# Two output products: making the last operands of a seven-product matmul inside its first group

## The chip, the cores and the metric

The kernel runs on one core of a Trainium2 chip. Its time is the device time of one execution in microseconds (us); three runs gave a median of 2010.18 us (2009.14 to 2012.45). The engines that matter here are TensorE (PE in the profile; its weight loads are PEld), VectorE (DVE), ScalarE (ACT), GpSimd (POOL) and SyncE (SP), which here only issues loads.

## The reference, cut to what matters

The reference is a small encoder trunk on an input x of 512 tokens by 2048 channels, all in float32. One layer (A) is a gated linear recurrence, one layer (B) is an attention with a forget gate; B takes its keys and values from the stream after A. Each layer ends in the same way, and only this end is touched:

```
o = head_rmsnorm(o, out_norm_w)              # 512 x 2048
o = o.reshape(B, T, D_MODEL) * silu(gate)
return x + (o @ w_out)                       # w_out: 2048 x 2048
```

There are two such output products, one per layer.

## The kernel before, in words

All activations lie transposed: 16 tiles of 128 channels by 512 tokens. For the matmuls each operand is split, in the type float32r, into a high part (ScalarE casts it: `xh`, `wh`) and a low part (VectorE subtracts the high part: `xl`, `wl`), and each product is made of three matmuls: high by high, low by high, high by low. Both steps of the split stand in the helper `split`, so all casts have line L444 and all subtractions L445, whatever they split.

An output product has two stages.

**The plain group.** `group` makes output rows 0 to 511 in the ordinary way: 16 contraction tiles, four banks `gm0` to `gm3`, three matmuls of 512 columns each, 192 matmuls (L242 to L244). Its callback `before(kt)` splits the activation tile `y{kt}` into `xh{kt}` and `xl{kt}`, and after each odd kt it calls `quick_prep` for the pair (kt-1, kt).

**Six seven-product groups.** The other 1536 output rows are made 256 at a time by a scheme that does a 2 by 2 block product with seven block products instead of eight. The contraction is cut into 8 pairs p of tiles. For each pair the scheme needs, beside quarters of the two activation tiles, three sums of quarters (`th{p}`, `tl{p}`) and a fourth that overwrites the second half of `xh`, `xl` of the even tile. `quick_prep` makes them: four subtractions of 128x256 on VectorE into a buffer `wm` (L261 to L264), then the split of three of them (128x768: `th`, `tl`) and of the fourth (128x256: into `xh`, `xl`). The weights come in chunks of 512 KB, each for two pairs: three coefficient blocks are used as loaded, four are sums. Per chunk, VectorE makes the sums (`w_sums`: L156 on 128x512, L157 and L158 on 128x256, into another `wm` buffer), and both kinds are split separately: the loaded ones as 128x768, the sums as 128x1024, all into the two tiles `w7h`, `w7l`. One pair is 21 matmuls of 256 columns (L296 to L298), one group 168, a product's six groups 1008. At the end of each group `quick_sum` combines the seven results on VectorE.

**Buffers.** Weights as loaded (`wr`) have two buffers, `w7h` and `w7l` two each, `wm` two, which operands and weight sums share. A chunk's load can start only when the chunk two before has been read; a split into `w7h` can start only when PE has finished with the chunk two before.

**What sets the order.** The program is written as one stream; a scheduler puts it into an order on each engine before the kernel is built, by its own estimate of when things are ready. Within an engine the order is then fixed: an instruction that waits holds all that stand behind it on that engine. In `quick`, the load of a chunk, its split, and then the matmuls are written pair by pair; the callback `make` of the change is called between the split and the matmuls.

## Time and profile before

| | |
|---|---|
| median of 3 runs | 2010.18 us |
| the profiled execution | 2011.1 us |
| its span | 2009.4 us |
| mean granted PE clock over the span | 0.995 |
| PE busy | 98% of the span |
| VectorE busy | 78% |
| ScalarE busy | 56% |
| PE share of the chain that ended last | 83% |

The span runs from the first to the last recorded instruction; 1.7 us of the execution lie outside it. A timeline row reads: start in us, duration in us, engine, line, operation, output <- input, shape, count, and in square brackets the engine's idle time before it with what ended it. On PE and VectorE the next instruction starts somewhat before the one ahead has ended, so what counts in a sequence is the distance from start to start. The seven-product groups of the first output product lie at 893 to 1028 us, those of the second at 1869 to 2002 us.

### The profile page before, as it was taken

The numbers are of one execution on the slowest core, as the hardware profiler recorded it, in microseconds if no ns is written. First come the engines' busy times: TensorE is split into PE (matmuls) and PEld (weight loads), VectorE is DVE, ScalarE is ACT, GpSimd is POOL, SyncE is SP. The second block draws the span as 40 slices with busy tenths as digits, with TensorE's granted clock in tenths as the row PEclk, the third lists the DMA queues.
The fourth block names the chain that finished last, engine by engine and source line by source line (L and its number), as shares of the span: only waits on it lengthen the run. The fifth ranks groups of instructions, "written<-read, shape, count | busy, mean of one in ns | idle before, by whom it ended". The sixth has DMA issues, their size and how long they took to land.

```text
span 2009.4 us, 28900 instructions
## 1 busy us (share of the span) xinstructions
PE 1978.4 (98%) x10218; PEld 1695.3 (84%) x10218; DVE 1558.7 (78%) x3321; ACT 1130.1 (56%) x2311; POOL 207.3 (10%) x365
## 2 busy tenths in 40 slices
PE   9999999999999999989999999999999999999898
PEld 7888888888888888879987888888888888888898
DVE  7969987979798889797893677776766676687877
ACT  6646655657566466653464555665555556576332
POOL 3303110203122030010000000000000000000100
PEclk9999999999999999999999999999999999999999
DMA  5222222222222222243432222322223332323443
GB/s 190 74 88 81 74 84 74 84 78 80 83 76 74 74 84 84 84 155 120 157 118 95 95 87 87 95 90 94 85 89 90 94 95 90 90 84 106 137 157 105
DMA packets 57600, 195.01 MB, mean 97 GB/s; under 512 B 7904, under 2 KB 8032, under 8 KB 57456
## 3 DMA queue, kind: packets, MB, share of 16 engines
q1 hardware_dynamic: 52192, 176.39, 28.0%
q0 software_dynamic: 5120, 16.78, 2.5%
q8 instruction: 80, 1.31, 0.3%
q14 instruction: 64, 0.52, 0.1%
q10 hardware_dynamic: 144, 0.01, 0.0%
HBM read 184.73 MB, written 8.42 MB: 96 GB/s over the span
## 4 chain that ended last, share of the span: by engine, by line
PE 83%; DVE 7%; DMA 5%; issue 3%; ACT 1%; POOL 1%; SPq 0%; POOLq 0%; DVEq 0%; ACTq 0%
PE gm L244 17%; PE gm L242 17%; PE gm L243 17%; PE gm L238 6%; PE gm L240 6%; PE gm L239 6%; DMA wr<-in_wa_q 3%; DVE w7l L445 2%; PE mx L594 2%; PE mx L593 2%; PE mx L592 1%; DMA wr<-in_wb_q 1%; PE mx L439 1%; PE mx L440 1%; PE mx L438 1%
## 5 line engine op out<-in xcount | busy, mean ns | idle before, releaser
L242 PE MATMUL gm<-xh,wh 128*128 128x512 f32 x1664 | 650.5, 392 | 0.1
L243 PE MATMUL gm<-xl,wh 128*128 128x512 f32 x1664 | 650.2, 391 | 0.0
L244 PE MATMUL gm<-xh,wl 128*128 128x512 f32 x1664 | 610.8, 392 | 0.2 <-DVE wl L445 0.2
L243 PEld LDWEIGHTS gm<-xl,wh 128*128 128x128 f32 x1664 | 313.2, 188 | 62.8
L242 PEld LDWEIGHTS gm<-xh,wh 128*128 128x128 f32 x1664 | 313.3, 188 | 62.6 <-DVE z L390 0.3
L244 PEld LDWEIGHTS gm<-xh,wl 128*128 128x128 f32 x1664 | 312.0, 188 | 62.6 <-DVE wl L445 0.9
L444 ACT CAST wh<-wr 128x512 fp32r<-128x512 f32 x288 | 177.3, 621 | 155.2 <-PE gm L243 112.7
L445 DVE TENSOR_TENSOR wl<-wr,wh 128x512 fp32r<-128x512 f32 x288 | 204.8, 714 | 67.2 <-ACT wh L444 57.3
L147 ACT ACTIVATE wh<-wr,v_b_norm_w 128x256 fp32r<-128x256 f32 (+1 forms) x192 | 111.6, 584 | 187.1 <-PE gm L243 152.1
L148 DVE SCALAR_TENSOR_TENSOR wl<-wr,v_b_norm_w,wh 128x256 fp32r<-128x256 f32 (+1 forms) x192 | 109.3, 570 | 131.6 <-ACT wh L147 126.4
L239 PE MATMUL gm<-wl,xh 128*128 128x512 f32 x512 | 200.2, 392 | 0.0
L240 PE MATMUL gm<-wh,xl 128*128 128x512 f32 x512 | 199.3, 392 | 0.0
L238 PE MATMUL gm<-wh,xh 128*128 128x512 f32 x512 | 179.6, 393 | 2.4 <-DVE q L556 1.6
L147 ACT ACTIVATE wh<-wr,v_kv_norm_w 128x256 fp32r<-128x256 f32 (+1 forms) x192 | 110.0, 573 | 56.1 <-PE gm L240 44.1
L148 DVE SCALAR_TENSOR_TENSOR wl<-wr,v_kv_norm_w,wh 128x256 fp32r<-128x256 f32 (+1 forms) x192 | 109.2, 570 | 32.7 <-ACT wh L147 32.1
L587 DVE COPY_PREDICATED at<-masks,mx 128x128 f32<-128x128 uint8 (+4 forms) x448 | 108.4, 296 | 13.6 <-PE mx L594 13.2
L238 PEld LDWEIGHTS gm<-wh,xh 128*128 128x128 f32 x512 | 95.8, 188 | 22.1 <-DVE q L556 1.9
L240 PEld LDWEIGHTS gm<-wh,xl 128*128 128x128 f32 x512 | 96.2, 188 | 19.0
L239 PEld LDWEIGHTS gm<-wl,xh 128*128 128x128 f32 x512 | 96.3, 188 | 18.8
L953 POOL TENSOR_SCALAR_AFFINE_SELECT s<-s 128x128 f32<-128x128 f32 x64 | 28.4, 444 | 741.6 <-DVE s L952 741.1
L444 ACT CAST w7h<-wr 128x768 fp32r<-128x768 f32 x48 | 40.1, 835 | 114.5 <-PE mx L297 48.8
L444 ACT CAST kh<-k 128x512 fp32r<-128x512 f32 (+1 forms) x96 | 56.4, 587 | 44.2 <-PE mx L593 19.0
(232 smaller groups left out, 3879.8 us busy)
## 6 DMA issues: line engine op xcount, KB each, us to landing
wr<-in_wb_qk SPq DMA_DIRECT2D x64, 512.0 KB, 3.5
wr<-in_wa_qf SPq DMA_DIRECT2D x62, 512.0 KB, 3.5
wr<-in_wa_v SPq DMA_DIRECT2D x32, 512.0 KB, 3.5
wr<-in_wa_g SPq DMA_DIRECT2D x32, 512.0 KB, 3.5
wr<-in_wb_v SPq DMA_DIRECT2D x32, 512.0 KB, 3.6
wr<-in_wb_g SPq DMA_DIRECT2D x32, 512.0 KB, 3.5
wr<-in_wa_q SPq DMA_DIRECT2D x24, 512.0 KB, 3.5
wr<-in_wb_q SPq DMA_DIRECT2D x24, 512.0 KB, 3.6
```

What stands on the lines that cost most here:

```text
L147: S.activation(h[:, c], r[:, c], AF.Copy, scale=w[:, kt : kt + 1])
L148: V.scalar_tensor_tensor(l[:, c], r[:, c], w[:, kt : kt + 1], rd(h)[:, c], op0=ALU.mult, op1=ALU.subtract)
L238: PE.matmul(banks[j], xh, h, start=f, stop=False)
L239: PE.matmul(banks[j], xh, l, start=False, stop=False)
L240: PE.matmul(banks[j], xl, h, start=False, stop=e)
L242: PE.matmul(banks[j], h[:, c], Xh[kt], start=f, stop=False)
L243: PE.matmul(banks[j], h[:, c], Xl[kt], start=False, stop=False)
L244: PE.matmul(banks[j], l[:, c], Xh[kt], start=False, stop=e)
L444: S.copy(h, src)
L445: return V.tensor_sub(l, src, rd(h))
L587: V.copy_predicated(out, mv, data)
L593: PE.matmul(lv[:, base : base + n], kh[:, c], ml, start=False, stop=False)
```

## The change

In the plain group the callback now makes the operands of pairs 0 to 4 only (after kt 1, 3, 5, 7 and 9). Those of pairs 5, 6 and 7 are made in the first seven-product group, one in each of its first three pair steps, between the weight split and the matmuls of that step. No arithmetic is added or removed, and each operand is still made by the same instructions.

```
     def quick(banks, prep, evac, hold, make=None):
...
             if not (wts.parts or hold and p == KT // 2 - 1):
                 wts.split()
+            if make:
+                make()
             th, tl, _ = prep[p]
...
-            end = quick(banks, prep, lambda *p, k=k, r=r: evac(k, r, p), hold and u == 5)
+            end = quick(banks, prep, lambda *p, k=k, r=r: evac(k, r, p), hold and u == 5, None if u else make)
...
+        def make():
+
+            if len(prep) < KT // 2:
+                prep.append(quick_prep(len(prep), Yd))
+                prep[-1][2]()
+
         def before(kt):
             y_split(kt)
-            if kt % 2:
-                prep.append(quick_prep(kt // 2, Yd))
-                prep[-1][2]()
+            if kt % 2 and kt < 10:
+                make()
```

The scheduler turns this into another order around the border between the two stages of each output product, and nowhere else. In the rows below, buffers have their numbers. The first weight chunk of the first output product is `wr_1873`, `w7h_1896`, `w7l_1897` before and `wr_1870`, `w7h_1887`, `w7l_1888` after; the second is `w7h_1904` before and `w7h_1898` after; the third, fourth and fifth are `w7h_1908`, `w7h_1912` and `w7h_1916` in both. Lines from the first edit on are two higher after the change (the split is L446 and L447).

VectorE at the border of the first output product, before: the last two of the four additions that empty the plain group's banks, the last two operands, and then the sums of the first two weight chunks together.

```order
L824 TENSOR_TENSOR y2_1920_9950<-gm2_1797_9288,z_1790_9275 128x512
L824 TENSOR_TENSOR y3_1921_9953<-gm3_1798_9289,z_1791_9277 128x512
L445 TENSOR_TENSOR tl6_1882_9644<-wm_1880_9638,th6_1881_9643 128x768
L445 TENSOR_TENSOR tl7_1894_9697<-wm_1892_9691,th7_1893_9696 128x768
L156 TENSOR_TENSOR wm_1895_9702<-wr_1873_9612 128x2x256
L156 TENSOR_TENSOR wm_1903_9751<-wr_1885_9665 128x2x256
L157 TENSOR_TENSOR wm_1895_9702<-wm_1895_9702,wr_1873_9612 128x2x128
L157 TENSOR_TENSOR wm_1903_9751<-wm_1903_9751,wr_1885_9665 128x2x128
L158 TENSOR_TENSOR wm_1895_9702<-wm_1895_9702,wr_1873_9612 128x2x128
L158 TENSOR_TENSOR wm_1903_9751<-wm_1903_9751,wr_1885_9665 128x2x128
L445 TENSOR_TENSOR w7l_1897_9707<-wm_1895_9702,w7h_1896_9706 128x2x512
L445 TENSOR_TENSOR w7l_1905_9756<-wm_1903_9751,w7h_1904_9755 128x2x512
```

The same engine after the change, from the last subtraction of pair 4 on: the first chunk's sums and both of its splits stand here, ahead of the low parts of pair 5, and the four additions come after four more rows.

```order
L264 TENSOR_TENSOR wm_1856_9532<-y9_1114_5706,wm_1856_9532 128x256
L156 TENSOR_TENSOR wm_1886_9669<-wr_1870_9601 128x2x256
L447 TENSOR_TENSOR w7l_1888_9674<-wr_1870_9601,w7h_1887_9673 128x2x384
L157 TENSOR_TENSOR wm_1886_9669<-wm_1886_9669,wr_1870_9601 128x2x128
L447 TENSOR_TENSOR wl_1883_9650<-wr_1861_9559,wh_1882_9649 128x512
L447 TENSOR_TENSOR tl4_1858_9538<-wm_1856_9532,th4_1857_9537 128x768
L158 TENSOR_TENSOR wm_1886_9669<-wm_1886_9669,wr_1870_9601 128x2x128
L261 TENSOR_TENSOR wm_1894_9697<-y10_1236_6344 128x256
L262 TENSOR_TENSOR wm_1894_9697<-y10_1236_6344,y11_1331_6803 128x256
L263 TENSOR_TENSOR wm_1894_9697<-y11_1331_6803,wm_1894_9697 128x256
L264 TENSOR_TENSOR wm_1894_9697<-y11_1331_6803,wm_1894_9697 128x256
L447 TENSOR_TENSOR w7l_1888_9674<-wm_1886_9669,w7h_1887_9673 128x2x512
```

ScalarE at the same border, before and after. `w7h<-wr` casts a chunk's loaded coefficients, `w7h<-wm` its sums.

```order
L444 CAST xh14_1886_9667<-wm_1892_9691 128x256
L444 CAST th6_1881_9643<-wm_1880_9638 128x768
L444 CAST th7_1893_9696<-wm_1892_9691 128x768
L444 CAST w7h_1896_9706<-wm_1895_9702 128x2x512
L444 CAST w7h_1904_9755<-wm_1903_9751 128x2x512
L444 CAST w7h_1908_9809<-wr_1902_9728 128x2x384
L444 CAST w7h_1908_9809<-wm_1907_9805 128x2x512
L444 CAST w7h_1912_9863<-wr_1906_9782 128x2x384
```

```order
L446 CAST w7h_1908_9809<-wr_1893_9695 128x2x384
L446 CAST w7h_1898_9733<-wm_1897_9729 128x2x512
L446 CAST th6_1901_9744<-wm_1900_9739 128x768
L446 CAST xh14_1880_9645<-wm_1904_9773 128x256
L446 CAST w7h_1912_9863<-wr_1903_9771 128x2x384
L446 CAST th7_1905_9778<-wm_1904_9773 128x768
L446 CAST w7h_1908_9809<-wm_1907_9805 128x2x512
L446 CAST w7h_1912_9863<-wm_1911_9859 128x2x512
L446 CAST w7h_1916_9917<-wr_1910_9836 128x2x384
```

In the order after, the cast of the third chunk's loaded coefficients stands ahead of the cast of the second chunk's sums, and the fourth's ahead of the third's; before, no cast of a later chunk's loaded coefficients stood ahead of an earlier chunk's sums in these rows.

VectorE after the change, some 20 rows behind the four additions:

```order
L447 TENSOR_TENSOR w7l_1913_9864<-wr_1903_9771,w7h_1912_9863 128x2x384
L447 TENSOR_TENSOR tl7_1906_9779<-wm_1904_9773,th7_1905_9778 128x768
L447 TENSOR_TENSOR w7l_1909_9810<-wm_1907_9805,w7h_1908_9809 128x2x512
L156 TENSOR_TENSOR wm_1911_9859<-wr_1903_9771 128x2x256
L156 TENSOR_TENSOR wm_1915_9913<-wr_1910_9836 128x2x256
L157 TENSOR_TENSOR wm_1911_9859<-wm_1911_9859,wr_1903_9771 128x2x128
L157 TENSOR_TENSOR wm_1915_9913<-wm_1915_9913,wr_1910_9836 128x2x128
L158 TENSOR_TENSOR wm_1911_9859<-wm_1911_9859,wr_1903_9771 128x2x128
L158 TENSOR_TENSOR wm_1915_9913<-wm_1915_9913,wr_1910_9836 128x2x128
L447 TENSOR_TENSOR w7l_1913_9864<-wm_1911_9859,w7h_1912_9863 128x2x512
```

Here too the fourth chunk's coefficients and the last operand stand ahead of the low part of the third chunk's sums, and the first sum of the fifth chunk stands ahead of the last two of the fourth. The second output product has the same order with other buffer numbers.

More of the change, by code (lines that the diff above doesn't have):

```diff
@@ L268, in quick_prep, with quick @@
         return th, tl, lambda: split(m[:, 0, :], Xh[k1][:, TN:], Xl[k1][:, TN:])
-    def quick(banks, prep, evac, hold):
+    def quick(banks, prep, evac, hold, make=None):
         half = lambda i: banks[i // 2][:, (i % 2) * TN : (i % 2 + 1) * TN]
@@ L315, in quick_sum, with quick_groups @@
         V.tensor_add(o2, d, r2)
-    def quick_groups(prep, first, residual, evac, hold):
+    def quick_groups(prep, make, first, residual, evac, hold):
         for u in range(6):
@@ L844, in out_product @@
         prep = []
+        def make():
+            if len(prep) < KT // 2:
+                prep.append(quick_prep(len(prep), Yd))
+                prep[-1][2]()
         def before(kt):
             y_split(kt)
-            if kt % 2:
-                prep.append(quick_prep(kt // 2, Yd))
-                prep[-1][2]()
+            if kt % 2 and kt < 10:
+                make()
         banks = group(None, before=before)
-        return quick_groups(prep, lambda: [evac0(j, banks[j]) for j in range(4)], residual, evac, hold)
+        return quick_groups(prep, make, lambda: [evac0(j, banks[j]) for j in range(4)], residual, evac, hold)
     last_a = out_product(out_a_evac(), res_a, quick_a, "oa", True)
```

## The prediction

> **What bounds the kernel now.** I read the page first, then who waited for whom on PE.
>
> ```profile
> PE 1978.4 (98%) x10218; PEld 1695.3 (84%) x10218; DVE 1558.7 (78%) x3321; ACT 1130.1 (56%) x2311; POOL 207.3 (10%) x365
> ```
>
> ```profile
> PE mx L296 <- ACT w7h L444: 14.3, 2, 7.5
> ...
> PE mx L298 <- DVE w7l L445: 2.0, 6, 0.5
> ```
>
> PE is busy 98% of the span, and 14.3 us of what it waits lie in two places: the first seven-product group of either output product, where it waits for ScalarE's cast `w7h` (columns: total, times, longest). The waits of `mx` matmuls for VectorE's low part are half a microsecond at most (one of 1.07 us in a `gm` bank comes below). PE's timeline there, first output product:
>
> ```profile
> 893.01 0.28 PE L296 MATMUL mx<-xh,w7h 128*128 128x256 f32 x1
> ...
> 893.96 0.28 PE L298 MATMUL mx<-xh,w7l 128*128 128x256 f32 x1
> 901.09 0.58 PE L296 MATMUL mx<-th,w7h 128*128 128x256 f32 x1 [6.85 <-ACT w7h L444]
> 901.48 0.42 PE L297 MATMUL mx<-tl,w7h 128*128 128x256 f32 x1
> 901.69 0.41 PE L296 MATMUL mx<-xh,w7h 128*128 128x256 f32 x1
> ...
> 905.05 0.28 PE L296 MATMUL mx<-th,w7h 128*128 128x256 f32 x1
> 905.17 0.28 PE L297 MATMUL mx<-tl,w7h 128*128 128x256 f32 x1
> ...
> 906.59 0.28 PE L297 MATMUL mx<-tl,w7h 128*128 128x256 f32 x1
> ...
> 921.95 0.28 PE L296 MATMUL gm<-xh,w7h 128*128 128x256 f32 x1
> ```
>
> Nine matmuls run 0.12 us apart (893.01 to 893.96), the tenth has to wait for the cast until 901.09, and from there to 905.05 they stand 0.21 us apart: the clock has fallen. The second group begins at 921.95. So the first group took 921.95 - 893.01 = 28.94 us, where its 168 matmuls at 0.12 us are 20.16 us: 8.78 us lost, 7.0 in the wait (894.09, where the tenth would start, to 901.09) and 1.8 at the slow clock. The second product:
>
> ```profile
> 1869.03 0.28 PE L296 MATMUL mx<-xh,w7h 128*128 128x256 f32 x1
> ...
> 1877.72 0.58 PE L296 MATMUL mx<-th,w7h 128*128 128x256 f32 x1 [7.45 <-ACT w7h L444]
> ...
> 1881.26 0.28 PE L297 MATMUL mx<-tl,w7h 128*128 128x256 f32 x1
> ...
> 1898.41 0.28 PE L296 MATMUL gm<-xh,w7h 128*128 128x256 f32 x1
> ```
>
> That is 29.38 us, 9.22 us lost. Both together, 18.0 us, are all that there is to win at this place. Why the cast was late is on VectorE and ScalarE:
>
> ```profile
> 883.41 0.42 DVE L445 TENSOR_TENSOR xl<-wm,xh 128x256 fp32r<-128x256 f32 x1
> ...
> 891.33 0.96 DVE L445 TENSOR_TENSOR w7l<-wr,w7h 128x768 fp32r<-128x768 f32 x1
> ...
> 893.21 0.68 DVE L824 TENSOR_TENSOR y<-gm,z 128x512 f32<-128x512 f32 x1
> 893.81 0.41 DVE L264 TENSOR_TENSOR wm<-y,wm 128x256 f32<-128x256 f32 x1
> 894.14 1.88 DVE L824 TENSOR_TENSOR y<-gm,z 128x512 f32<-128x512 f32 x3
> 895.94 1.81 DVE L445 TENSOR_TENSOR tl<-wm,th 128x768 fp32r<-128x768 f32 x2
> 897.67 1.28 DVE L156 TENSOR_TENSOR wm<-wr 128x512 f32<-128x512 f32 x2
> 898.88 0.75 DVE L157 TENSOR_TENSOR wm<-wm,wr 128x256 f32<-128x256 f32 x2
> 899.55 0.75 DVE L158 TENSOR_TENSOR wm<-wm,wr 128x256 f32<-128x256 f32 x2
> 901.07 2.36 DVE L445 TENSOR_TENSOR w7l<-wm,w7h 128x1024 fp32r<-128x1024 f32 x2 [0.77 <-ACT w7h L444]
> ```
>
> ```profile
> 884.38 0.85 ACT L444 CAST w7h<-wr 128x768 fp32r<-128x768 f32 x1 [1.31 <-DMA wr<-in_wa_q]
> ...
> 890.40 0.84 ACT L444 CAST w7h<-wr 128x768 fp32r<-128x768 f32 x1 [2.38 <-DMA wr<-in_wa_q]
> ...
> 900.00 1.99 ACT L444 CAST w7h<-wm 128x1024 fp32r<-128x1024 f32 x2 [4.91 <-DVE wm L158]
> 906.91 0.84 ACT L444 CAST w7h<-wr 128x768 fp32r<-128x768 f32 x1 [4.93 <-DVE wm L157]
> ```
>
> The first chunk had landed by 884.38, yet VectorE sums it (L156) only at 897.67, behind all operands and the four additions; the cast of the sums follows at 900.00. It is an order, no lack of data.
>
> **The change, part by part.** No instruction is added or removed. From VectorE's rows I take the distances from start to start: 0.34 us for 128x256 (two of L157 in 0.67), 0.60 for L156 and for an addition, 0.87 for a 128x768 split (`tl`, `w7l<-wr`), 1.14 for `w7l<-wm` (lasting 1.22). ScalarE's casts take 0.84 (next start 0.74 later) and 1.04 (0.95). The orders differ from the row at 883.41 on. First product:
>
> *First chunk.* L264 at 883.75; L156 at 884.4, when the load is there; coefficients 885.3; L157 886.1; the last plain weight split 886.5 (0.34 later than before); `tl4` 887.1; L158 887.9, done 888.35; ScalarE's cast of the sums 888.4 to 889.45; VectorE makes four subtractions meanwhile and then the low part, to 890.85. PE wants them from 893.7 on. The wait of 7.0 us and the slow clock go, with over 3 us to spare.
>
> *Second chunk.* Loads:
>
> ```profile
> 886.84 3.53 DMA wr<-in_wa_q
> ...
> 900.42 5.08 DMA wr<-in_wa_q
> ...
> 929.62 6.55 DMA wr<-in_wa_q
> ```
>
> The second load waits for that plain split, so it is issued at 887.2 instead of 886.84 and lands at 890.7; its cast ends 891.6. VectorE: its coefficients 891.6, L156 892.5, `tl5` 893.1, the four additions 893.97 to 896.4, then L157, two subtractions and L158, done 897.8. But ScalarE has the third chunk's coefficients ahead of these sums, and that cast waits for PE to finish reading chunk one. The row at 906.59 is that last read before the change; it ends 906.87, and the cast starts at 906.91. Now the last read is the 41st matmul: 893.01 + 40 x 0.12 + 0.28 = 898.09, cast at 898.13, so the second chunk's sums are cast 898.87 to 899.91. PE has begun pair 2 at 898.05 and can do nine matmuls, to 899.13: it waits **0.83 us**. Eight more, to 900.92; the low part, behind the third chunk's coefficients on VectorE (899.0), runs 899.94 to 901.16: **0.28 us**. The other 25 matmuls of pairs 2 and 3 end the stretch at 904.20.
>
> *Third chunk.* VectorE from 901.08: `tl6`, two subtractions, L156, then L263, `xl14`, L157, L264 and L158, done 904.99. ScalarE again first casts the next chunk's coefficients, released by PE at 901.20 + 23 x 0.12 + 0.28 = 904.24; then `th7` at 905.02; the third chunk's sums 905.76 to 906.81. PE is there at 905.28: **1.58 us**. Eight matmuls, 907.82; the low part, behind `w7l_1913` and `tl7`, ends 908.11: **0.33 us**. 25 more, to 911.15.
>
> *Fourth chunk.* The fifth load goes out when L158 frees its buffer (905.05) and lands 3.5 us later, 908.6; its L156 stands ahead of the fourth chunk's last sums, which so end at 910.39, cast 911.48, low part 912.73. PE wants them at 912.23 and 913.91: no wait, 0.75 and 1.2 us to spare. What covers this is the load's 3.5 us.
>
> Sum: 3.02 us, so the group takes 23.18 us and the second begins 28.94 - 23.18 = **5.76 us** earlier. In the second product the chunks come thus:
>
> ```profile
> 1860.98 0.84 ACT L444 CAST w7h<-wr 128x768 fp32r<-128x768 f32 x1 [2.19 <-DMA wr<-in_wb_q]
> ...
> 1867.08 0.84 ACT L444 CAST w7h<-wr 128x768 fp32r<-128x768 f32 x1 [2.47 <-DMA wr<-in_wb_q]
> ```
>
> The first is there 8.05 us ahead of PE's first matmul (1869.03), against 893.01 - 884.38 = 8.63 above: 0.58 us less. The same working gives 0.84, 0.59, 1.58 and 0.34: only the second low part feels it, since the other waits hang on PE's own release. 3.35 us, so 29.38 - 23.51 = **5.87 us**.
>
> All else moves earlier as it is. First the busy times over a stretch (PE, PEld, DVE, ACT, POOL, then the granted clock), then PE at the end of the first product:
>
> ```profile
> 932.00:1022.00 90.00, 88.48 (x725) 87.06 (x723) 73.32 (x117) 38.60 (x47) 7.59 (x14) 1.00 0.45 143
> ```
>
> ```profile
> 1024.62 0.38 PE L298 MATMUL gm<-th,w7l 128*128 128x256 f32 x1 [1.07 <-DVE w7l L445]
> ...
> 1027.71 0.40 PE L238 MATMUL gm<-wh,xh 128*128 128x512 f32 x1
> ```
>
> VectorE is busy 73.32 of 90 us over the later groups, so a lead lost in the first is made up there; and what those groups lose already (921.95 to 1027.71 is 105.8 us for 840 matmuls, 100.8 at 0.12) stays, since their order stays from the middle of the second group on. The additions now start at 893.97 instead of 893.21; behind their stores stand the residual loads, and those are needed only when the first group ends.
>
> The unknown is the clock after shorter waits. The row at 1024.62 ends a wait of 1.07 us, and the plain group follows at full distance: no price. After 7.0 us it cost 1.8 us. The waits of 1.58 us are nearest the first; I take nothing, and keep 1.8 us for each product as the other end. The Trainium skill ("TensorE: Matmul & The Clock Gate", Part 1) says that the clock halves after at least one idle window of about 3.4 us, and that the window runs free; by this rule none of the four waits costs anything, the sum stays, and the two rows quoted agree with it.
>
> Sum: 5.76 + 5.87 = 11.6 us off the profiled execution's 2011.1 is 1999.5. The median ran 0.9 us below that execution, so **1998.6**.
>
> **Rivals.** *Everything is covered*: all 18.0 us, 1992.2. For it: the first chunk's 3 us to spare. Against: two casts wait for PE itself, so part of the waits is built into the order. *Part is given back*: the clock falls after the 1.58 us waits (3.6 us in both), or VectorE, whose work from the additions to the fifth chunk's low part adds up to 19.7 us by these distances, as much as PE's 20.16, trails into the second group, and PE waits there a few more times by the half microsecond of the row for L298; 2002 to 2005. *VectorE bounds the whole product*, and what the first group wins its later groups lose: 2010. Against it stands the row from 932 to 1022. *Slower, by the loads*: after the change the third, fourth and fifth chunk's loads each go out only when sums in the new order free a buffer, beside the additions' stores. A load took 3.53 us alone, 5.08 beside another, and once 6.55. A late one holds VectorE at L156 ahead of the fourth chunk's sums. With all three at 6.55, 9.1 us per product are lost against the 5.8 won: 2010.2 + 2 x 3.3 = 2016.8; it ends slower from about 5.5 us per load, if none of that is hidden. Against: the third and fourth have 2 us or more of cover, so only the fifth counts in full.
>
> **How the numbers follow.** Forecast 0.60, with 1995.4 to 2001.8 its own range (waits half or one and a half times the 6.4 us, clock free); all covered 0.10; part given back 0.20; nothing 0.05; slower 0.05. The range from 1993.5 to 2004.5 leaves out most of the full cover, the worst of the part given back, and the last two. A measurement of this kernel tells about 0.2%, 4 us, from no change. Faster by more, below 2006.2: 0.60 + 0.10 + 0.19, 0.89. Same: the rest of that case, 0.05, and 0.01 of the slower one, 0.07. Slower 0.04.
>
> **What would show it.** In the profile after: no wait near 7 us before a `mx` matmul at L298; a first group of about 23.2 us instead of 28.9, with two waits near 0.8 and 1.6 us for `w7h` and two near 0.3 for `w7l`; PE's granted clock at 1.00 there; ScalarE's cast of the second and third chunk's sums right behind one that waited for PE. I am wrong if a wait stands before the fourth chunk, if the slow spacing of 0.21 us returns, or if the groups from the second on take more than the 105.8 us of now.

## The result

The changed kernel takes 1996.57 us (median of 4 runs, 1994.76 to 1998.31), the kernel before 2010.38 us beside it (4 runs, 2009.14 to 2012.45): a ratio of 0.9933 [0.9918, 0.9948], 13.8 us less. The forecast was 1998.6 us, 2.0 us above the measured median. The profiled execution took 1994.76 us, its span 1993.1 us; the granted clock over the span is 0.999 instead of 0.995.

The view of waits after the change (the waiter, what it waited for, total us, times, longest) no longer has a wait near 7 us:

```profile
PE mx L298 <- ACT w7h L446: 4.4, 4, 1.4
...
PE gm L300 <- DVE w7l L447: 1.1, 1, 1.1
```

The 14.3 us for `w7h` in two waits are 4.4 us in four. PE's timeline, the first group of either product and the end of the first product (lines are two higher than before):

```profile
893.30 0.28 PE L298 MATMUL mx<-xh,w7h 128*128 128x256 f32 x1
...
900.29 0.38 PE L298 MATMUL mx<-th,w7h 128*128 128x256 f32 x1 [0.72 <-ACT w7h L446]
900.52 0.28 PE L299 MATMUL mx<-tl,w7h 128*128 128x256 f32 x1
...
907.34 0.39 PE L298 MATMUL mx<-th,w7h 128*128 128x256 f32 x1 [1.45 <-ACT w7h L446]
...
916.81 0.28 PE L298 MATMUL mx<-xh,w7h 128*128 128x256 f32 x1
...
1019.47 0.40 PE L238 MATMUL gm<-wh,xh 128*128 128x512 f32 x1
...
1860.79 0.28 PE L298 MATMUL mx<-xh,w7h 128*128 128x256 f32 x1
...
1867.85 0.38 PE L298 MATMUL mx<-th,w7h 128*128 128x256 f32 x1 [0.78 <-ACT w7h L446]
...
1869.35 0.38 PE L300 MATMUL mx<-th,w7l 128*128 128x256 f32 x1 [0.29 <-DVE w7l L447]
...
1875.13 0.39 PE L298 MATMUL mx<-th,w7h 128*128 128x256 f32 x1 [1.45 <-ACT w7h L446]
...
1884.59 0.28 PE L298 MATMUL mx<-xh,w7h 128*128 128x256 f32 x1
```

The row at 916.81 is the 169th matmul, the one at 1019.47 the first after the product. So the first groups took 23.51 and 23.80 us, of which 20.16 are work. ScalarE's casts behind the two longer waits in the first product:

```profile
888.64 1.05 ACT L446 CAST w7h<-wm 128x1024 fp32r<-128x1024 f32 x1 [1.91 <-DVE wm L158]
...
898.46 0.84 ACT L446 CAST w7h<-wr 128x768 fp32r<-128x768 f32 x1 [0.60 <-PE mx L299]
899.20 1.04 ACT L446 CAST w7h<-wm 128x1024 fp32r<-128x1024 f32 x1
...
904.78 0.84 ACT L446 CAST w7h<-wr 128x768 fp32r<-128x768 f32 x1 [1.64 <-PE mx L299]
906.25 1.04 ACT L446 CAST w7h<-wm 128x1024 fp32r<-128x1024 f32 x1
```

The first chunk's sums are cast at 888.64, 11.4 us earlier than before. The casts at 898.46 and 904.78 waited for PE, and the sums of the second and the third chunk stand behind them (899.20, 906.25). And the busy times of PE, PEld, DVE, ACT, POOL in two stretches with the granted clock behind them:

```profile
898.00:902.00 4.00, 3.23 (x25) 2.82 (x24) 3.71 (x7) 2.52 (x3) 1.48 (x3) 1.00 0.96 320
...
906.00:910.00 4.00, 2.55 (x19) 2.34 (x20) 4.00 (x6) 1.29 (x2) 0.00 (x0) 1.00 0.38 131
```

The clock is 1.00 in both, with waits of 0.72 and 1.45 us inside.

For this kernel and all that follow, the table gives what each profiled execution lost in the seven-product groups: the time from one matmul to the 168th behind it less 168 x 0.12 us, summed for groups 2 to 6. It goes by count, since after the change matmuls of the second group stand among the last of the first. In three kernels some of the plain group's matmuls stand in the first group (four in either product with four pairs moved; four and twelve with GpSimd); they are work and are taken off, 0.227 us each. Span less losses is 1983.7 us before and 1983.9 us after, so these losses hold the whole difference.

| kernel | median of the runs, us | ratio to before | first group, product 1 / 2 | groups 2 to 6, product 1 / 2 | span |
|---|---|---|---|---|---|
| before | 2010.38 | 1 | 8.78 / 9.22 | 4.96 / 2.78 | 2009.4 |
| after | 1996.57 | 0.9933 | 3.35 / 3.64 | 1.86 / 0.30 | 1993.1 |
| change in one product only | 2002.37 | 0.9957 | 3.34 / 9.68 | 1.02 / 2.86 | 2000.7 |
| first sums first, operands not moved | 1999.63 | 0.9942 | 4.46 / 6.41 | 3.85 / 2.67 | 2001.2 |
| before, PE kept running (6.6 us of extra matmuls taken off in each first group) | 2011.12 | 1.0002 | 8.0 / 7.8 | 6.1 / 2.65 | 2008.4 |
| before, one row of VectorE moved | 2008.14 | 0.9986 | 9.41 / 8.98 | 2.64 / 3.23 | 2008.3 |
| before, quiet queues | 2009.37 | 0.9995 | 9.67 / 9.19 | 2.36 / 3.12 | 2007.3 |
| after, loud queues | 2000.52 | 0.9948 | 3.33 / 3.65 | 8.16 / 0.40 | 1998.8 |
| after, casts in turn | 1996.86 | 0.9930 | 4.35 / 4.52 | 2.15 / 2.23 | 1996.6 |
| four pairs moved | 1999.04 | 0.9942 | 4.85 / 4.60 | 2.35 / 0.14 | 1995.8 |
| before, subtractions on GpSimd | 2006.61 | 0.9981 | 6.60 / 8.00 | 2.62 / 1.24 | 2003.6 |
| the same with casts in turn, after the change | 2003.72 | 0.9965 | 6.12 / 6.61 | 2.28 / 2.06 | 2002.6 |
| after, additions behind | 1992.51 | 0.9915 | 1.0 / 1.42 | 4.09 / 0.34 | 1990.8 |

From before to after the first groups gained 5.43 and 5.58 us, 11.0 together, where 5.76 and 5.87 were forecast. The later groups gained 3.10 and 2.48 us, 5.6 together, where nothing was forecast. Most of that, 5.0 us, lies in groups 2 and 3, which lost 0.86 and 1.76 us in the first product before, 0.63 and 1.77 in the second, and nothing after. That is the question that the result leaves.

### The profile page after: what moved, and what is told of

Its sections match the earlier page's. It is cut to its first block, busy times and chain, and to the rows that moved or that the text cites. A ratio compares the mean times of both kernels' runs of the same rounds, so it can differ in the third digit from the quotient of the medians.

```text
span 1993.1 us, 28895 instructions
## 1 busy us (share of the span) xinstructions
PE 1973.4 (99%) x10218; PEld 1690.8 (85%) x10218; DVE 1557.6 (78%) x3321; ACT 1128.9 (57%) x2311; POOL 207.6 (10%) x365
## 4 chain that ended last, share of the span: by engine, by line
PE 87%; DVE 6%; DMA 3%; issue 2%; ACT 1%; POOL 1%; SPq 0%; POOLq 0%; DVEq 0%; ACTq 0%
PE gm L244 18%; PE gm L242 17%; PE gm L243 17%; PE gm L238 6%; PE gm L240 6%; PE gm L239 6%; PE mx L596 2%; PE mx L595 2%; PE mx L594 1%; DVE w7l L447 1%; DMA wr<-in_wa_q 1%; PE mx L300 1%; PE mx L299 1%; PE mx L298 1%; PE gm L300 1%
## 5 line engine op out<-in xcount | busy, mean ns | idle before, releaser
L446 ACT CAST wh<-wr 128x512 fp32r<-128x512 f32 x288 | 177.2, 620 | 154.2 <-PE gm L243 112.4
L447 DVE TENSOR_TENSOR wl<-wr,wh 128x512 fp32r<-128x512 f32 x288 | 204.4, 713 | 66.8 <-ACT wh L446 57.1
L446 ACT CAST w7h<-wr 128x768 fp32r<-128x768 f32 x48 | 40.1, 835 | 94.4 <-PE mx L299 43.0
L446 ACT CAST kh<-k 128x512 fp32r<-128x512 f32 (+1 forms) x96 | 56.4, 587 | 44.2 <-PE mx L595 19.0
```

Of the source, the lines that this page charges most:

```text
L446: S.copy(h, src)
L447: return V.tensor_sub(l, src, rd(h))
```

## Experiments

Each kernel was timed beside the kernel before on the same chip; the medians of before were 2010.48, 2010.14, 2010.57 and 2010.02 us for the four sets. In some diffs `tc.issue_after(a)` stands: it puts an instruction behind `a` in the order of the engine, without a wait. In these kernels lines are shifted by what was inserted.

**The change in one product only.** Is the gain each product's own?

```
-            if kt % 2 and kt < 10:
+            if kt % 2 and (kt < 10 or not hold):
                 make()
```

> The change in the first output product only; the second is made as before. If the gain is made in each product for itself (first group about 5.4 us, later groups about 3 us), the first product ends 8.2 us earlier than before and the second is again 133 us long, with a wait of about 7.4 us in its first group and 2.8 us lost in its later groups: 2010.4 - 8.2 = 2002.2. If the second product gains from what the first leaves behind, its first group's wait is shorter without its own edit, and the time is nearer 1997.

Measured: 2002.37 us (2001.03 to 2003.54), ratio 0.9957 [0.9944, 0.9969]. The first product lost 3.34 us in its first group, as after the change, the second 9.68, as before, and the longest wait is back, once:

```profile
PE mx L298 <- ACT w7h L446: 9.3, 3, 7.1
```

The two halves are separate: 8.1 us of the 13.8 come with the first product alone.

**The first chunk's sums first, operands not moved.** The change moves operands, and the sums of the first weight chunk come forward with that. Which of the two counts? Here all operands are made in the plain group as before, and the program asks for the first sums after kt 13.

```
+        def early(self):
+            for n, (fn, c) in enumerate(self.raw):
+                if c == 2:
+                    parts = fn()
+                    self.raw[n] = (lambda: parts, c)
+                    return
...
             y_split(kt)
+            if kt == 13:
+                wts.early()
```

> Before, with all operands made in the plain group as before, but the first chunk's sums and splits written ahead of the operands of pair 6. Theory: what the first group gains depends on where the first chunk's sums stand on VectorE and not on where the operands are made. By the distances of the rows, PE then waits about 0.6 us for the first chunk's low part region, 2.2, 1.6 and 0.3 us for the rest, 4.7 us in place of 8.8 in the first product and about 5 in place of 9.2 in the second: 8.3 us less, 2002. If the order in the second group is what the later groups gained by, this kernel has that too (the low part of the last coefficients stands ahead there), 5 us more: 1997. Rival: the operands' place is what counts, since seven operand instructions more lie ahead of the additions; the first group keeps a wait over 5 us and the time stays above 2005.

Measured: 1999.63 us (1998.05 to 2002.92), ratio 0.9942 [0.9929, 0.9956]: 10.9 us of the 13.8. Its waits:

```profile
PE mx L305 <- DVE w7l L452: 4.6, 7, 1.6
PE mx L303 <- ACT w7h L451: 4.6, 4, 1.5
```

Neither wait of 7 us is left, though every operand is still asked for in the plain group: the first chunk's sums are cast at 893.07 instead of 900.00. So the place of the first sums on VectorE is the cause of that wait; the moved operands are the way in which the change reaches it. On one engine, what goes ahead pushes something behind: here pair 7's subtractions came behind the four additions (897.69 to 900.39). And the low part of the first chunk's sums, which the change puts ahead of the additions (889.99), stands behind them (895.69), so that PE waits 1.6 us for it. The median can't be divided by groups. The profiled execution, the slowest of the five, shows 7.1 us gained in the first groups and 1.2 in the later ones.

**Before, with PE kept running.** The 1.8 us at the slow clock were a term of the forecast. Here 55 extra matmuls (6.6 us at 0.12) into a bank that is not yet in use fill most of the 7 us wait; their result is overwritten.

```
                 o = half(i)
+                if fill and i == 1:
+                    for _ in range(55):
+                        PE.matmul(banks[3][:, :TN], h[:, 0, :], Xh[14][:, hi], start=True, stop=True)
```

> Before, with 55 matmuls of 256 columns more in each output product's first seven-product group behind its first three matmuls, into a bank whose contents are overwritten; they fill about 6.6 us of the long wait, so TensorE does not stand still there. Theory clock: the spacing of 0.21 us behind the wait (1.8 us in the first product, about 1.6 in the second) comes from standing still; with the fillers the spacing is 0.12 there, and the time 2010.4 - 3.4 = 2007.0. Rival: the spacing comes from something else at that place (operands or weights that arrive late); it stays, 2010.4, or more if the fillers run past the cast.

Measured: 2011.12 us (2009.08 to 2012.7), ratio 1.0002 [0.9993, 1.0011]: no change. The stretch from 901 to 905 us, before, then with the extra matmuls:

```profile
901.00:905.00 4.00, 3.91 (x18) 3.91 (x19) 3.06 (x3) 0.99 (x2) 0.00 (x0) 0.50 0.90 328
```

```profile
901.00:905.00 4.00, 3.59 (x28) 3.28 (x27) 2.36 (x2) 1.37 (x2) 0.00 (x0) 1.00 0.92 345
```

With PE running, the clock is 1.00 instead of 0.50 and 28 matmuls pass in place of 18: standing still is what brought the clock down. But the time did not move. In the trace, PE reaches the 31st matmul of the two first groups (extra ones not counted) 1.28 and 1.77 us sooner than before, 3.0 us together. By the end of these groups 0.8 and 1.4 us are left of it. In the first product the second group gives that back and more (groups 2 to 6 lost 1.1 us more than before); the second product keeps it. The waits of `mx` matmuls for VectorE's low parts, 2.0 us in six before, are

```profile
PE mx L302 <- DVE w7l L449: 1.8, 5, 0.5
```

so PE, at full speed, waits for VectorE about as often as before. The span of this execution is 1.0 us shorter than before's; by the interval, at most 1.4 us of the 3.0 reach the time. So the loss at the slow clock can't be added to the wait as if it were free to win by itself.

**Before, with one row of VectorE moved.** Where did the 5.6 us of the later groups come from? At the end of the second group VectorE before the change has this order, first product:

```profile
936.19 0.69 DVE L156 TENSOR_TENSOR wm<-wr 128x512 f32<-128x512 f32 x1 [4.07 <-DMA wr<-in_wa_q]
936.80 0.95 DVE L445 TENSOR_TENSOR w7l<-wr,w7h 128x768 fp32r<-128x768 f32 x1
```

and after the change:

```profile
927.88 0.96 DVE L447 TENSOR_TENSOR w7l<-wr,w7h 128x768 fp32r<-128x768 f32 x1 [1.16 <-ACT w7h L446]
...
929.21 0.69 DVE L156 TENSOR_TENSOR wm<-wr 128x512 f32<-128x512 f32 x1
```

Before, the first sum of the third group's first chunk (L156 at 936.19) waited 4.07 us for a load, and a low part of the second group's last chunk (936.80), which needs nothing of this load, stood behind it. After, the low part (927.88) stands ahead of that sum (929.21). The section on the change put the new order only around the border of the two stages, and the forecast only up to the middle of the second group; this pair of rows stands at that group's end. Here the kernel before gets that one pair of rows in the order of after, in each product:

```
-        V.tensor_add(m[:, :, 0:2, :], r[:, :, 2:4, :], view(r, 0, [[4 * P, 2], [0, 2], [1, P]]))
+        with tc.issue_after(low[-1]) if len(low) % 24 == 8 else ExitStack():
+            V.tensor_add(m[:, :, 0:2, :], r[:, :, 2:4, :], view(r, 0, [[4 * P, 2], [0, 2], [1, P]]))
```

> Before, with one rule more in each output product: on VectorE the first sum of the first chunk of the third group may be issued only behind the low part of the last coefficients of the second group (before, it stands ahead of it and waits 4.07 us for its load there; after the change it stands behind). The first group stays as before. Theory order: what the later groups gained, 3.1 us in the first product and 2.5 in the second, comes from this exchange; the waits of PE between 937 and 952 us go, and the time is 2010.4 - 5.6 = 2004.8 (2004 to 2007). Rival load: those groups gained because the load of that chunk no longer meets the stores and residual loads at the group border (6.55 us before); the order is no matter, the waits stay or move by a few tenths, 2010.4.

Measured: 2008.14 us (2004.51 to 2010.05), ratio 0.9986 [0.9977, 0.9995]: 2.8 us by the ratio. VectorE at the place:

```profile
934.11 0.96 DVE L168 TENSOR_TENSOR w7l<-wr,w7h 128x768 fp32r<-128x768 f32 x1 [0.96 <-ACT w7h L167]
936.63 0.69 DVE L159 TENSOR_TENSOR wm<-wr 128x512 f32<-128x512 f32 x1 [1.56 <-DMA wr<-in_wa_q]
```

The low part (934.11) no longer stands behind the wait for the load (936.63), and groups 2 and 3 of the first product lost nothing there, where they lost 0.86 and 1.76 us before. But groups 4 to 6 of that product lost 0.65, 0.61 and 1.38, and in the second product, where the row has moved too, groups 2 and 4 lost 0.84 and 1.79. The order of this one row is a cause at its place; the sum over all later groups fell from 7.74 to 5.87 us only.

**Before, with quiet queues.** The load that VectorE waited for was slow: 6.55 us. It went out at 929.62, behind two stores and two residual loads that GpSimd had issued from 926.72 to 929.35. This kernel leaves these transfers out, in the first product only: the first layer's output tiles from the fifth on are not stored, and residuals from the seventh tile on are not loaded. VectorE keeps before's order.

```
+        if kt > 5:
+            return kept[kt % 2]
...
-        nc.gpsimd.dma_start(x1_d[kt], X1[kt])
+        if kt < 4:
+            nc.gpsimd.dma_start(x1_d[kt], X1[kt])
```

> Before, without the stores of the stream after layer A from row tile 4 on and without the loads of residuals from row tile 6 on in the first output product; the additions there take the residual of row tile 4 or 5 instead, and layer B's residuals come from the input x from row tile 4 on. This part of the computation is left out. The order on VectorE and ScalarE in the first two groups of either product is that of before. Theory load: the waits of the second and third group of the first product (0.86 and 1.76 us lost in the trace before) come from the load at 929.62 that took 6.5 us behind the stores and residual loads of the group's border; without these it takes 3.5 us, and the two groups lose under 0.3 us together; the second product, which is not touched, loses what it lost. 2010.4 - 2.4 = 2008.0. Rival order: VectorE's order alone makes the loss; it stays at 2 us or more in these groups, 2010.4.

Measured: 2009.37 us (2008.4 to 2010.87), ratio 0.9995 [0.9986, 1.0004]. Groups 2 and 3 of the first product lost 0.00 and 0.07 us. The same load, by the view of transfers (the last number is us from issue to landing), first with the one row moved, then with quiet queues, then after the change:

```profile
wr<-in_wa_q SPq DMA_DIRECT2D x1, 512.0 KB, 6.0
```

```profile
wr<-in_wa_q SPq DMA_DIRECT2D x1, 512.0 KB, 3.4
```

```profile
wr<-in_wa_q SPq DMA_DIRECT2D x1, 512.0 KB, 4.5
```

So in these two runs either repair was enough at this place: with the order mended, a load of 6.0 us cost nothing; with the load at 3.4 us, the old order cost nothing. It is not enough in every run: the kernel with the first sums first has the better order there too (low part at 928.90, sum at 932.96), its load also took 6.0 us, and its groups 2 and 3 lost 0.79 and 0.61 us. After the change both hold, the better order and a load of 4.5 us, and which of them did it there was not separated. The other later groups keep losing now here, now there, so the gain in the timed runs is small, and "no change" is not excluded.

**After, with loud queues.** The other way round: after the change, two more stores of 256 KB each (output rows 4 and 5, written a second time) go out at that border of the first product.

```
         nc.gpsimd.dma_start(x1_d[kt], X1[kt])
+        if kt in (4, 5):
+            nc.gpsimd.dma_start(xx_d[kt - 4], X1[kt])
```

> After the change, with two stores more of 256 KB each at the border of the first and second group of the first output product (the same two row tiles once more, into memory that nothing reads). Theory load: the load that took 4.5 us there takes 6 us or more and the second or third group loses 1 to 2 us, though the order is that of after: 1996.6 + 1.5 = 1998.1. Rival order: with the low part of the last coefficients ahead of the sum that waits for the load, the two groups lose under 0.3 us even when the load takes over 6 us; 1996.6.

Measured: 2000.52 us (1997.53 to 2003.15), ratio 0.9948 [0.9936, 0.9961]; 9.6 us below before, where after was 13.8 below its own runs of before; the two intervals still overlap. At that border the extra stores did slow the load: issued at 924.12, it took 7.1 us instead of 4.5, and with the order of after group 2 lost 0.58 us. The larger loss is one border later, where no extra store goes out. The load issued at 946.84 among four ordinary transfers of GpSimd took 8.0 us (5.2 after the change). Both loads, then PE and VectorE behind the second:

```profile
wr<-in_wa_q SPq DMA_DIRECT2D x1, 512.0 KB, 7.1
```

```profile
wr<-in_wa_q SPq DMA_DIRECT2D x1, 512.0 KB, 8.0
```

```profile
956.74 0.58 PE L300 MATMUL mx<-th,w7l 128*128 128x256 f32 x1 [3.14 <-DVE w7l L447]
957.12 0.41 PE L300 MATMUL mx<-xh,w7l 128*128 128x256 f32 x1
957.33 0.41 PE L298 MATMUL mx<-xh,w7h 128*128 128x256 f32 x1
```

```profile
954.85 0.69 DVE L156 TENSOR_TENSOR wm<-wr 128x512 f32<-128x512 f32 x1 [5.24 <-DMA wr<-in_wa_q]
955.46 1.22 DVE L447 TENSOR_TENSOR w7l<-wm,w7h 128x1024 fp32r<-128x1024 f32 x1
```

Again a first sum (954.85) waits for its load ahead of a low part that PE needs (955.46). The change leaves this pair of rows in that order: after it, the sum at this place waited 1.02 us (950.02) and PE lost nothing. Here group 3 lost 6.05 us: the wait, and then the slow spacing (957.12 to 957.33 is 0.21 us). So the order of after is better at the first of these borders and not at the next, and there a slow load brings the loss back. Whether the extra stores also made the load at 946.84 slow is not shown.

**After, with the casts in turn.** Two waits of the forecast come from ScalarE's order, where a later chunk's coefficients stand ahead of an earlier chunk's sums. Here they stand behind, for the third and the fourth chunk.

```
+        with tc.issue_after(sums[-1]) if len(sums) % 24 in (2, 3) else ExitStack():
+            S.copy(h[:, :, 0:3, :], r[:, :, 1:4, :])
```

> After the change, with one rule more in each output product: ScalarE may cast the third and the fourth chunk's loaded coefficients only behind the cast of the chunk's sums ahead of them. After the change they stood ahead, waited there for TensorE to finish reading the chunk two before, and held the sums that TensorE wanted next; VectorE's low parts of those coefficients move behind in the same way. Theory: the four waits in the first group (0.72, 0.29, 1.45 and 0.34 us by the timeline, 3.5 us with the gaps around them in the first product, 3.6 in the second) come from that order; they shrink to about 0.5 us in each product: 1996.6 - 6 = 1990.6. Rival: VectorE, with 19.7 us of work for a group of 20.16 us, is the limit behind it; then the same time comes back as waits for VectorE's low parts in the first and second group, and the time stays at 1995 to 1997.

Measured: 1996.86 us (1994.01 to 1998.31), ratio 0.9930 [0.9916, 0.9943]: the time of after. The wait before the second chunk fell from 0.88 us to 0.1. But VectorE, busy 24.86 of the 26 us from 885 to 911, was right behind, and PE waited a chunk later:

```profile
905.99 0.39 PE L304 MATMUL mx<-th,w7h 128*128 128x256 f32 x1 [1.56 <-ACT w7h L170]
...
907.84 0.58 PE L306 MATMUL mx<-th,w7l 128*128 128x256 f32 x1 [0.63 <-DVE w7l L171]
```

```profile
904.00:906.00 2.00, 0.43 (x5) 0.23 (x3) 1.83 (x5) 1.90 (x3) 0.00 (x0) 1.00 0.26 96
906.00:908.00 2.00, 1.37 (x9) 1.16 (x9) 2.00 (x3) 0.68 (x1) 0.00 (x0) 0.85 0.79 252
908.00:910.00 2.00, 2.00 (x10) 2.00 (x11) 2.00 (x5) 0.04 (x1) 0.00 (x0) 0.50 0.00 0
```

After these two waits the clock was at 0.50, to which the single wait of 1.45 us after the change had not brought it. ScalarE's order and VectorE's work are two limits close together, and mending ScalarE's order alone was worth nothing.

**Four pairs moved.** One more pair than the change moves (pair 4 too).

```
-            if kt % 2 and kt < 10:
+            if kt % 2 and kt < 8:
                 make()
```

> The change with four pairs moved into the first group in place of three: the operands of pairs 4 to 7 are made there. Theory: the first sums were early enough with three (no wait for them, over 3 us to spare), so a fourth gains nothing at the first chunk; VectorE has 2.6 us more to do in the first group, 22.3 us for 20.16, and ScalarE's casts of the next chunk's coefficients stand ahead of the sums of the second, third and fourth chunk (after three pairs: of the second and third). The first group loses 5 to 6 us in place of 3.5: about 1996.6 + 4 = 2000.5. Rival: the earlier first chunk is worth more; the first group loses less than 3.5 us and the time is below 1995.

Measured: 1999.04 us (1997.54 to 2000.03), ratio 0.9942 [0.9930, 0.9955]. The interval and that of after overlap, so the slowdown by 2.5 us is not certain. In the trace the first groups lost 4.85 and 4.60 us, 1.5 and 1.0 more than with three pairs. In the first product the wait before the third chunk grew, since the cast of the fourth chunk's loaded coefficients (905.30), which stands ahead of the third's sums on ScalarE, waited for a load of 7.3 us; the clock stayed at 1.00 over it. In both products the low part of the fourth chunk's sums came late, which it had not with three pairs:

```profile
905.30 0.83 ACT L446 CAST w7h<-wr 128x768 fp32r<-128x768 f32 x1 [2.18 <-DMA wr<-in_wa_q]
```

```profile
907.87 0.39 PE L298 MATMUL mx<-th,w7h 128*128 128x256 f32 x1 [2.00 <-ACT w7h L446]
...
916.27 0.39 PE L300 MATMUL mx<-th,w7l 128*128 128x256 f32 x1 [0.34 <-DVE w7l L447]
```

```profile
904.00:906.00 2.00, 1.87 (x16) 1.66 (x14) 1.29 (x4) 0.69 (x1) 0.00 (x0) 1.00 0.31 123
906.00:908.00 2.00, 0.13 (x1) 0.13 (x2) 1.83 (x3) 1.82 (x3) 0.00 (x0) 1.00 0.74 229
```

So a fourth pair brings nothing at the first chunk and costs a new wait for VectorE in the first group, half a microsecond in each product with its steps. That is near the part of the second rival in which VectorE trails, but it does not reach the second group, which lost nothing in either product.

**Subtractions on GpSimd.** GpSimd is busy 10% of the span. Here the four subtractions of pairs 5, 6 and 7 run on it, in the kernel before, and in a second run in the one with the casts in turn.

```
+        if p >= 5:
+            G.tensor_sub(b11, b12, b11)
+            G.tensor_sub(b12, b12, b22)
+            G.tensor_sub(b22, b22, b11)
+            G.tensor_sub(b21, b21, b22)
```

> Before, without the change: the four subtractions of pairs 5, 6 and 7 are made on GpSimd in place of VectorE, into the tiles of the activations, which nobody reads afterwards; their splits stay on ScalarE and VectorE. GpSimd does them well ahead (in the order they stand in the middle of the plain group), so that VectorE has 3 x 4 x 0.34 = 4.1 us less to do at the border, and the first chunk's sums stand ahead of the additions there, as after the change. With the change's edit as well the order on all engines is the same as without. Theory: the first group is bound by what VectorE has to do between 885 and 912 us; with 4 to 7 us less of it there the long wait goes without moving anything, and of the waits there stay those that ScalarE's cast of the third chunk's loaded coefficients ahead of the second chunk's sums makes, about 0.8 us: first group 1 to 2 us lost in place of 8.8 and 9.2, 2010.4 - 15 = 1995 with the later groups as before, down to 1990 if these gain as after the change. Rival: GpSimd's subtractions slow VectorE or come late themselves; the first group still loses 5 us or more and the time is above 2001.

> After the change, with both: the subtractions of pairs 5, 6 and 7 on GpSimd, and ScalarE's casts of the third and fourth chunk's loaded coefficients behind those of the sums ahead. Theory VectorE: putting the casts in turn gave nothing by itself because VectorE had no room; with 4 us less on VectorE the waits of the first group go for good, under 1 us in each product: after's 1996.6 less 2 x 3 = 1990.6, or lower if the later groups lose nothing. Rival: another limit, the loads of the third and fourth chunk that take 6 to 7 us behind the stores and residual loads; then waits of 1 to 2 us stay before the third or fourth chunk and the time is 1993 to 1997.

Measured: 2006.61 us (2005.37 to 2009.04), ratio 0.9981 [0.9972, 0.9990], and 2003.72 us (2002.76 to 2004.7), ratio 0.9965 [0.9952, 0.9977]; the second is 7 us slower than the same casts without GpSimd. GpSimd and VectorE in the second kernel:

```profile
862.69 8.62 POOL L267 TENSOR_TENSOR y<-y 128x256 f32<-128x256 f32 x1 [1.04 <-DVE xl L466]
...
876.83 1.07 POOL L269 TENSOR_TENSOR y<-y,y 128x256 f32<-128x256 f32 x1
```

```profile
877.22 1.84 DVE L283 TENSOR_TENSOR wm<-y,wm 128x256 f32<-128x256 f32 x2
...
887.08 0.76 DVE L283 TENSOR_TENSOR wm<-y,wm 128x256 f32<-128x256 f32 x2
```

A subtraction of 128x256 took 0.74 to 1.12 us on GpSimd, once 8.62 us, against 0.42 on VectorE. And VectorE slowed beside it: two subtractions took 1.84 us at 877.22 and 0.76 us at 887.08, when GpSimd had finished. The operands came late, and some of the plain group's matmuls with them; how much of the loss each of the two slowdowns makes was not separated. The Trainium skill ("SBUF — State Buffer", section "SBUF: two separate sides") says that the two engines share a port pair and that a VectorE operation with two SBUF inputs and GpSimd exclude each other there; these rows agree.

**After, with the additions behind.** From the runs above: the casts in turn help only if VectorE is ahead too. The four additions that empty the plain group's banks take 2.4 us of VectorE in front of the second chunk's sums. This kernel has the casts in turn for the third to the fifth chunk, the additions behind the fourth chunk's last sum, and the fifth chunk's first sum behind that sum too.

```
-        V.tensor_add(m[:, :, 3, :], m[:, :, 2, :], r[:, :, 1, :])
+        last.append(V.tensor_add(m[:, :, 3, :], m[:, :, 2, :], r[:, :, 1, :]).ins)
...
+        with tc.issue_after(sums[-1]) if len(sums) % 24 in (2, 3, 4) else ExitStack():
+            S.copy(h[:, :, 0:3, :], r[:, :, 1:4, :])
...
-                first()
+                with tc.issue_after(last[len(last) // 24 * 24 + 3]):
+                    first()
```

> After the change, with ScalarE's casts in turn (third, fourth and fifth chunk) and the four additions that empty the plain group's banks issued on VectorE only behind the fourth chunk's sums, so behind the third chunk's low part, and with the fifth chunk's first sum behind the fourth's last. Nothing is taken off VectorE, but 2.4 us of it are moved out of the stretch where it was late (from 893.9 to about 906 us), and the stores and residual loads that follow the additions go out some 8 us later, so the fourth chunk's load no longer meets them. Theory VectorE: by the distances of the rows the second chunk's sums are cast by 896.4, the third's by 903.4 and the fourth's by 907, each ahead of TensorE; the first group loses under 0.8 us in each product in place of 3.5 and 3.6: 1996.6 - 2 x 2.9 = 1990.8, if the later groups lose what they lost after the change. Rival load: the stores and residual loads then meet the sixth or seventh chunk's load (6 us or more in place of 3.5), and the second group loses 1 to 3 us in each product: 1993 to 1997.

Measured: 1992.51 us (1991.92 to 1995.28), ratio 0.9915 [0.9901, 0.9928], the fastest of all. It was not timed beside after; its median is 4.1 us lower, and the two intervals overlap from 0.9918 to 0.9928. The first groups lost 1.0 and 1.42 us. VectorE:

```profile
904.09 1.22 DVE L171 TENSOR_TENSOR w7l<-wm,w7h 128x1024 fp32r<-128x1024 f32 x1
...
908.10 2.48 DVE L833 TENSOR_TENSOR y<-gm,z 128x512 f32<-128x512 f32 x4
```

The low part of the third chunk's sums starts at 904.09, 3.3 us ahead of its place after the change (907.39), and the additions at 908.10. With them, their stores and residual loads moved too, from the fourth chunk's load to the seventh's; these two loads, issued at about 895 and 913 us:

```profile
wr<-in_wa_q SPq DMA_DIRECT2D x1, 512.0 KB, 3.5
```

```profile
wr<-in_wa_q SPq DMA_DIRECT2D x1, 512.0 KB, 6.3
```

(With the casts in turn the fourth chunk's load took 6.8 us.) The slow load is only passed on: group 2 of the first product lost 0.85 us, of the second nothing. Three things were changed at once here (casts, additions, the fifth chunk's first sum), and what each is worth was not separated.

## Why the prediction was right, and where it was not

*The first wait and the slow clock go.* Right. The first chunk's sums were cast at 888.64 where 888.4 was forecast, and no wait stands before them. That the first sums' place in VectorE's order is the reason is shown by the run that asked for them earlier and left the operands in the plain group. That the slow clock follows from standing still is shown by the run with extra matmuls; that its 1.8 us could be won by themselves was not borne out, for with the clock at 1.00 and the wait filled the time stayed (ratio 1.0002). Counted together with the wait, as the sum did, it made no error.

*The second and third chunk.* Right in place and cause: the casts at 898.46 and 904.78 (forecast 898.13 and 904.24) waited for PE and held the sums. The steps from start to start lost 0.88, 0.20, 1.61 and 0.27 us in the first product (forecast 0.83, 0.28, 1.58, 0.33) and 0.94, 0.45, 1.60 and 0.26 in the second (0.84, 0.59, 1.58, 0.34). That makes 2.96 and 3.25 us against 3.02 and 3.35. **A term was missing:** after each wait the first step is longer too (900.29 to 900.52 is 0.23 us instead of 0.12), about 0.11 us for each of the four, 0.4 us per product. With it the sums are 3.4 and 3.7 us; the groups lost 3.35 and 3.64.

*The fourth chunk: no wait.* Right, though a load was late: the fourth chunk's took 6.3 us behind the additions' transfers, and ScalarE's cast of it (904.78) still waited for PE and not for the load. The cover named for it, "2 us or more", held. The slower rival, that all three loads cost in full, didn't come.

*The clock after shorter waits: no price.* Right for this kernel: 1.00 in 898 to 902 and 906 to 910. The reason was too simple. Waits of 1.56 and 0.63 us with some work between them did bring it down in another kernel, so the length of one wait doesn't decide.

*VectorE, 19.7 us against PE's 20.16.* The warning was right and the place of it open. After the change it does not trail into the second group, which lost nothing. With the casts in turn it is the limit in the first, and with a fourth pair it makes one more wait there.

*"What those groups lose already ... stays, since their order stays from the middle of the second group on."* **This is the step that failed.** Groups 2 to 6 lost 2.16 us instead of 7.74 in the profiled execution. The order had changed at the second group's end, one row of VectorE, and the loads went out at other times against GpSimd's transfers. At that place two conditions had met before, a first sum ahead of a needed low part and a load of 6.55 us for that sum; taking away either one removed the loss there in the first product. In time, each alone is worth little: 2.8 us [1.0, 4.6] and 1.0 us [-0.8, 2.8] by their ratios. What after gained over its forecast was less in the median than in the trace as well: 2.0 us instead of 4.7, since its profiled execution was the fastest of its four. The first groups' 11.0 us and the median's 13.8 us leave about 3 us for the later groups.

So it was partly luck that the number came so close, by two errors of opposite sign: the first groups gave 0.6 us less than forecast and the later ones more. Open remain which of the two conditions counts in the changed kernel itself, and why the later groups' losses move from place to place between executions. Not all of them hang on loads. Group 6 of the first product lost 1.0 to 2.0 us in every kernel of the table. After the change PE waits there 1.14 us (1016.38) for a low part that stands on VectorE behind operands of the next layer, and the group's last load took 3.5 us.

## What to carry to other kernels

Where an engine waits seven microseconds for something whose data has long been there, look for what stands ahead of it on the engine that makes it; here asking for the first chunk's sums earlier was worth 10.9 us by the medians, where the whole change was worth 13.8. Before counting a second loss behind the first (a slow clock, a cast out of turn), ask which engine is next in line: here VectorE stood so close behind PE and ScalarE that mending ScalarE's order alone gave nothing, and moving VectorE's additions out of the way as well gave 4 us by the medians, with intervals that still overlap. A change of order moves transfers as well, and their durations in the later stages are part of the sum.

## What the runs showed of the hardware

- **The granted clock fell at two waits close together, and not at a single one of 2.00 us.** In the kernel with the casts in turn PE waited 1.56 and 0.63 us between 904.4 and 907.8, and the clock fell to 0.50 from 907.39 to 910.80, 3.41 us; the second product shows 0.50 for 3.41 us too (1876.78 to 1880.19), behind two such waits. PE was busy 1.66 of the 3.41 us before the first fall. Over a single wait of 2.00 us (four pairs moved) the clock stayed at 1.00, in one of 3.14 us (loud queues) it fell. The slow stretch before the change, which began in the wait of 6.85 us, lasted 6.83 us (898.14 to 904.97). By what rule the clock falls, and whether the two kernels differ only by when their waits began, these runs do not show. The Trainium skill ("TensorE: Matmul & The Clock Gate", Part 1) asks for at least one idle window of about 3.4 us; the first case, where PE worked between the two waits, doesn't agree with that, and the measurement decides.
- **A load of 512 KB took 3.4 to 8.0 us, longer among other transfers.** Away from GpSimd's transfers of 256 KB it took 3.4 and 3.5 us, issued among or right behind them, in the places looked at, 4.5 to 7.3 (7.1 with two more stores), and once 8.0 among no more than four of them. So their number alone does not give the time.
- **GpSimd beside VectorE costs VectorE.** The same 128x256 subtraction went from 0.38 us in a row of two (0.76 at 887.08) to 0.92 (1.84 at 877.22), and one on GpSimd took 8.62 us beside a run of VectorE operations.
